# Two early blocks of the first expert, and another order of the experts' turns, in a fused transformer and mixture-of-experts layer

## The chip, the cores and the metric

The kernel runs on one core of a Trainium2 chip. The metric is the device time of one execution in microseconds (us). A core has a matrix engine (TensorE, PE in the rows; its weight loads are PEld), a vector engine (VectorE, DVE), an activation engine (ScalarE, ACT), a general engine (GpSimd, POOL) and a queue engine that issues most transfers (SyncE, SP). Each runs its own instructions in a fixed order, and they wait for each other through semaphores.

## The reference, cut to what matters

One layer on 2,048 tokens of width 1,024: attention and a gated MLP are mixed and projected, the result is normalised and modulated (h2), and h2 goes through a mixture of 32 experts of which each token uses two. What an expert does with its tokens:

```python
    def run_block(args):
        xt, e = args
        hid = jax.nn.silu(xt @ w1[e]) * (xt @ w3[e])
        return hid @ w2[e]
    y = lax.map(run_block, (xb, blk_e)).reshape(cap, d)
    out = jnp.zeros_like(t).at[buf_tok].add(y * buf_w[:, None])
    ...
    x = _layernorm(ALPHA * x + g2 * _hier_moe(h2, lp), ln2_g[i], ln2_b[i])
```

Each expert has 6 MB of weights in fp32 (w1, w3: 1,024 x 512, w2: 512 x 1,024).

## The kernel before

`pass1` computes the projections and the attention, `pass2` the mixing, the norms and the routing of the tokens, `moe` the experts, `final` the last norm. Routing writes, for each expert, a list of its tokens and their weights to `tok_d`; `moe_tables` ranks the experts by their number of tokens, and `CAPS` says how many rows each rank computes (448 down to 64; what does not fit goes through a slow loop, `further_blocks`).

**The end of pass2.** `first_expert` picks the expert that has the most tokens in the first twelve of sixteen token tiles. `early_block` takes 128 of its tokens, which are known before the routing ends, and puts their work between that of the last four tiles (`last_tiles`): it gathers their rows of h2, multiplies by w1 and w3 in plain fp32 (L987, tiles `mm<-mraw,ex`), gates, multiplies by w2, scales (`result`, L1029) and adds into `acc_d`. The order of this stretch is made by a planner (`Plan`) from hand-given durations. The expert's list is then moved forward by 128 places, so that `moe` sees only the rest.

**The turns of moe.** `ORDER` lists the ranks in the order in which they get their turn; rank 0 is the expert of the early block. A turn has one to four blocks of 128 rows; where the rows of a rank end on 64, the last block has 64 rows. For each block i the program runs `hidden(i)` (48 matmuls of 128x512, 32 for a 64-row block), the transposes of the gate of block i-1, `gate(i)` (silu on ACT, products on DVE), `rows(i+1)` (8 transposes of the next block's gathered rows, split into a high and a low part), `output(i-1)` (24 matmuls, or 16) and `evacuate(i-1)` (DVE scales the result, for 64 rows GpSimd also multiplies by g2, then a GpSimd transfer adds the rows into `acc_d`).

**The weights.** An expert's weights come as six pieces of 1 MB into eight buffers `mraw` (RAWS = 8). `prepare` splits each piece into a high part (`mWh`, a cast on ACT) and a low part (`mWl`, a subtraction on DVE, both at L84) and then issues the next load. There are six places for split pieces, so pieces 0 to 3 of the next expert are split during the last block of this one, as `hidden` gives their places free, and pieces 4 and 5 in the block after, behind `output`:

```python
            if last:
                prepare(s + 1, 3)
            if i and blocks[i - 1][3]:
                prepare(s, 4)
                prepare(s, 5)
```

**The start of moe.** SP reads the ranked experts' numbers, loads the token lists (L1519, which waits until the last of the routing's writes to `tok_d` has landed) and two weight pieces (L1530); GpSimd gathers three blocks of rows (L1565); `rows(0)` needs the first of them. The tiles: `xg` gathered rows, `xh`/`xl` their split transposes, `hs` the gated hidden rows, `gh`/`gl` their split transposes, `yo` a scaled result. L1579 and L1586 are the transposes of 128-row and 64-row blocks, L1600 is every matmul of an expert.

Of the kernel before, what the change touches and what calls it, by code (L numbers as in the profile page):

```python
# [703 lines left out]
def pass2(k):  # L704
    nc, tc, T = k.nc, k.tc, k.T
    k.late = k.ctx.enter_context(tc.tile_pool(name="late", bufs=1, reuse_waits="tile"))
    with ExitStack() as ctx:
# [245 lines left out]
        def early_block(plan, ends, done):  # L953
# [4 lines left out]
            lst = k.late.tile([P, 2], I32, name="elst")  # L958
            nc.sync.dma_start(lst, k.tok_d[bass.ds(e, 1), 0:P, :].rearrange("o p w -> p (o w)"))
# [58 lines left out]
            turn, take = rows(lambda: E["hs"], 0, (wk, "vg", 2))  # L1018
# [6 lines left out]
            def result(h):  # L1025
                if h == 0:
                    E["yo"] = k.late.tile([P, D], F32, name="eyo", tag="yo", bufs=1)
                sl = slice(h * 512, (h + 1) * 512)
                nc.vector.scalar_tensor_tensor(E["yo"][:, sl], E["y", h], lst.bitcast(F32)[:, 1:2], E["g2"][:, sl],  # L1029
                                               op0=OP.mult, op1=OP.mult)  # L1030

            def store():
                tc.keep_in_program_order(nc.gpsimd.indirect_dma_start(
                    out=k.acc_d[0:(nb + 1) * P, :], out_offset=bass.IndirectOffsetOnAxis(ap=lst[:, 0:1], axis=0),
                    in_=E["yo"], in_offset=None, compute_op=OP.add))
            d = [add("DVE", 0.65, lambda h=h: result(h), d) for h in range(2)]
            add("Pool", 1.0, store, *d, *done[:4])

# [458 lines left out]
def moe(k):  # L1497
    nc, tc, T = k.nc, k.tc, k.T
    with ExitStack() as ctx:
# [32 lines left out]

        def prepare(s, p):
# [336 lines left out]
```

## Time and profile before

| | |
|---|---|
| median of 3 runs | 2368.75 us (2363.58 to 2372.4) |
| the profiled execution | 2368.24 us, span of its instructions 2366.1 us |
| PE busy | 2206.7 us, 93% of the span |
| DVE, ACT, GpSimd busy | 1739.7, 1196.1, 662.7 us |
| weight pieces of the experts | 192 of 1,024 KB |
| first and last transposes and matmuls of moe | 1496.15 us, about 2303 us |

A busy time is the sum of an engine's instructions; how much of it can be shortened is told only by the rows of one stretch, which stand below.

### The profile page before, as it was taken

Reading aid. Unit: us, or ns where it says so; the run is one execution under the profiler, and the core shown is the slowest. Engines: PE = TensorE matmul, PEld = TensorE weight load, DVE = VectorE, ACT = ScalarE, POOL = GpSimd, SP = SyncE. Lnnn points to the kernel's source line nnn. Section 1 sums busy time; section 2 is a strip of 40 time slices with the busy share of each in tenths; the row PEclk is TensorE's granted clock in tenths of the full one; section 3 lists DMA queues with packets and bytes.
Section 4 is the critical chain, followed back from the end, with each engine's and each line's share of the span. In section 5 each row is a group of like instructions: output and inputs, shape, how many; then the busy total and the mean of one; then the engine's idle time right before and its main releaser. Section 6 shows DMA issues by size and latency. Waiting matters only on the chain. (4 is left out here: it accounts for less than half of the span.)

```text
span 2366.1 us, 31837 instructions
## 1 busy us (share of the span) xinstructions
PE 2206.7 (93%) x11269; PEld 1811.8 (77%) x11269; DVE 1739.7 (74%) x3029; ACT 1196.1 (51%) x1673; POOL 662.7 (28%) x518
## 2 busy tenths in 40 slices
PE   7899999999999999999999998899999998999980
PEld 3799898897788788878877886677777786777770
DVE  4778888887675777578557858489786968658977
ACT  3566666666332334333333333367665756546655
POOL 1333333331000101011101113234363636224424
PEclk9999999999999999999999998899999999999995
DMA  8111111115574445544445435699998989768967
GB/s 311 63 59 59 59 54 41 41 46 198 186 245 139 160 147 178 156 143 152 134 127 162 148 94 191 209 329 340 303 352 273 332 246 334 252 195 310 361 184 293
DMA packets 126853, 449.86 MB, mean 190 GB/s; under 512 B 20778, under 2 KB 42210, under 8 KB 102116
## 3 DMA queue, kind: packets, MB, share of 16 engines
q1 hardware_dynamic: 113828, 405.82, 49.2%
q0 software_dynamic: 12864, 41.98, 7.8%
q8 instruction: 90, 1.47, 0.2%
q14 instruction: 71, 0.58, 0.1%
HBM read 383.18 MB, written 64.57 MB: 189 GB/s over the span
## 5 line engine op out<-in xcount | busy, mean ns | idle before, releaser
L84 DVE TENSOR_TENSOR mWl<-mraw,mWh 128x2048 fp32r<-128x2048 f32 x192 | 437.5, 2311 | 57.6 <-ACT mWh L84 56.8
L84 ACT CAST mWh<-mraw 128x2048 fp32r<-128x2048 f32 x192 | 360.2, 1912 | 108.5 <-PE h L1600 79.1
L99 POOL TENSOR_TENSOR mv<-mv,mhalf 128x1 f32<-128x1 f32 x58 | 60.2, 1040 | 663.7 <-DVE mv L98 657.4
L84 DVE TENSOR_TENSOR Wl<-raw,Wh 128x1024 fp32r<-128x1024 f32 x140 | 170.5, 1220 | 77.4 <-ACT Wh L84 77.0
L1600 PE MATMUL h<-mWh,xh 128*128 128x512 f32 x784 | 217.9, 398 | 3.8 <-ACT xh L84 2.5
L84 ACT CAST Wh<-raw 128x1024 fp32r<-128x1024 f32 x140 | 146.1, 1048 | 139.6 <-PE mm L742 67.3
L1600 PE MATMUL h<-mWl,xh 128*128 128x512 f32 x784 | 210.9, 390 | 0.0
L741 PE MATMUL mm<-hh,Wl 128*128 128x512 f32 x512 | 201.8, 394 | 6.6 <-DVE Wl L84 6.6
L740 PE MATMUL mm<-hh,Wh 128*128 128x512 f32 x512 | 203.3, 397 | 2.5 <-ACT Wh L84 1.9
L742 PE MATMUL mm<-hl,Wh 128*128 128x512 f32 x512 | 201.5, 393 | 0.0
L1647 POOL DMA_INDIRECT acc_d<-yo,lst x49 | 141.3, 2883 | 194.0 <-DVE yo L1641 132.4
L1600 PEld LDWEIGHTS h<-mWl,xh 128*128 128x128 f32 x784 | 147.5, 188 | 31.7
L1600 PEld LDWEIGHTS h<-mWh,xh 128*128 128x128 f32 x784 | 144.2, 189 | 35.1 <-ACT xh L84 3.3
L1646 POOL TENSOR_TENSOR yo<-yo,g2b 64x1024 f32<-64x1024 f32 x20 | 119.9, 5997 | 127.4 <-DVE yo L1644 119.6
L382 PE MATMUL pj<-wq,hTh 128*128 128x256 f32 (+1 forms) x544 | 150.3, 352 | 1.7 <-DVE hTh L363 1.6
L1600 PE MATMUL h<-mWh,xl 128*128 128x512 f32 x464 | 126.7, 394 | 5.5 <-DVE xl L84 5.4
L84 ACT CAST ph<-pt 128x512 fp32r<-128x512 f32 x184 | 93.4, 520 | 73.3 <-PE pt L571 69.8
L547 ACT ACTIVATE Sb<-Sb,mx 128x641 f32<-128x641 f32 (+1 forms) x128 | 105.4, 823 | 40.5 <-DVE mx L542 31.5
L1600 PE MATMUL y<-mWh,gh 128*128 128x512 f32 x392 | 112.7, 407 | 13.1 <-DVE gh L84 11.7
L540 DVE CUSTOM_DVE_ANT_0 Sb<-S,mask,sink 128x640 f32<-128x640 f32 (+1 forms) x128 | 110.3, 862 | 18.9 <-PE S L536 16.1
L84 DVE TENSOR_TENSOR pl<-pt,ph 128x512 fp32r<-128x512 f32 x184 | 109.1, 605 | 19.1 <-ACT ph L84 17.2
L1565 POOL DMA_INDIRECT xg<-h_d,lst x49 | 76.9, 1569 | 163.2 <-PE tr L1579 81.3
(379 smaller groups left out, 5393.1 us busy)
## 6 DMA issues: line engine op xcount, KB each, us to landing
mraw<-mw SPq DMA_DIRECT2D x192, 1024.0 KB
raw<-wf SPq DMA_DIRECT2D x96, 512.0 KB
raw<-ada SPq DMA_DIRECT2D x32, 512.0 KB
raw<-wo SPq DMA_DIRECT2D x32, 512.0 KB
x<-x SPq DMA_DIRECT2D x30, 512.0 KB
x<-ada SPq DMA_DIRECT2D x16, 512.0 KB
hT_d<-hf SPq DMA_DIRECT2D x32, 256.0 KB
raw<-hT_d SPq DMA_DIRECT2D x16, 512.0 KB
```

The lines of the kernel that those rows point to most:

```text
L84: return k.nc.scalar.copy(hi, src), (eng or k.nc.vector).tensor_sub(lo, src, hi)
L99: nc.gpsimd.tensor_tensor(mv[:, 3:4], mv[:, 2:3], k.mhalf, op=OP.pow)
L382: ins = nc.tensor.matmul(box[0][:, :n], x[:, kc, ts], wpart(y, kc, slice(c0, c0 + n))[:, 0, :], start=q == 0, stop=q == 3 * KC - 1)
L540: nc.vector.tensor_tensor_reduce(x[:, :nk], S[:, :nk], mask[:, mi, :nk], 1.0, sink[:, h:h + 1], OP.add, OP.max, mx[:, s:s + 1])
L547: nc.scalar.activation(Sb[s][:, :nk + 1], Sb[s][:, :nk + 1], AF.Exp, bias=mx[:, 2 + s:3 + s], scale=1.0, accum_out=mx[:, 4 + s:5 + s])
L740: nc.tensor.matmul(out, lh, rh, start=first, stop=False)
L741: nc.tensor.matmul(out, ll, rh, start=False, stop=False)
L742: nc.tensor.matmul(out, lh, rl, start=False, stop=last)
L1565: ins = nc.gpsimd.indirect_dma_start(out=xg[i][0:n, :], out_offset=None, in_=k.h2_d[:, :], in_offset=bass.IndirectOffsetOnAxis(ap=lists[s] ...
L1600: nc.tensor.matmul(accs[m], a[:, ks], b[:, c0:c0 + 512], start=first and i + j == 0, stop=last and j == 1 and i == len(t) - 1)
L1646: nc.gpsimd.tensor_tensor(yo[0:64], yo[0:64], g2[0:64], op=OP.mult)
L1647: nc.gpsimd.indirect_dma_start(out=k.acc_d[:, :], out_offset=bass.IndirectOffsetOnAxis(ap=l[0:n, j, 0:1], axis=0), in_=yo[0:n, :], in_offs ...
```

## The change

1. `early_block` loads and gathers 256 tokens of the first expert: the first 128 into `xg` as before, the next 128 into a tile of their own, `k.xg0`. The list is moved forward by 256 places, and the rows of rank 0 go from 384 to 256.
2. The second half of the early block's work (the product with w2, its scaling and its store) leaves `early_block` and becomes `early_output` at the start of `moe`. Its operand waits in `k.early`, in one of the eight `mraw` buffers; so one weight piece fewer is loaded at the start of `moe`, and it follows in the second block's step.
3. The second 128 tokens become block 0 of `moe`, whose rows come from `k.xg0`. `moe` has 49 blocks as before, and `pass2` works on one.
4. Places of tiles: the split pieces get a place each by their number, and some tiles are named first, which sets where they lie in memory.
5. In a turn of more than two blocks with 64 rows left over, the block of 64 rows comes second and not last.
6. Another `ORDER`.

```diff
             e = nc.sync.value_load(k.e0[0:1, 0:1], min_val=0, max_val=31)
-            lst = k.late.tile([P, 2], I32, name="elst")
-            nc.sync.dma_start(lst, k.tok_d[bass.ds(e, 1), 0:P, :].rearrange("o p w -> p (o w)"))
+            k.elst = k.late.tile([P, 2, 2], I32, name="elst")
+            nc.sync.dma_start(k.elst, k.tok_d[bass.ds(e, 1), 0:2 * P, :].rearrange("o (b p) w -> p (o b) w", p=P))
...
-            nc.sync.dma_start(rest, move(1))
+            nc.sync.dma_start(rest, move(2))
             nc.sync.dma_start(move(0), rest)
             xg = whole(wk, "rr", 4)
-            nc.gpsimd.indirect_dma_start(out=xg, out_offset=None, in_=k.h2_d[0:(nb + 1) * P, :],
-                                         in_offset=bass.IndirectOffsetOnAxis(ap=lst[:, 0:1], axis=0))
+            k.xg0 = k.late.tile([P, D], F32, name="xg0", tag="yo", bufs=1)
+            for b, x in enumerate((xg, k.xg0)):
+                nc.gpsimd.indirect_dma_start(out=x, out_offset=None, in_=k.h2_d[0:(nb + 1) * P, :],
+                                             in_offset=bass.IndirectOffsetOnAxis(ap=k.elst[:, b, 0:1], axis=0))
...
-                E["g2"] = whole(wk, "rr", 4)
-                nc.sync.dma_start(E["g2"], bcast_row(k.g2_d[0], D))
...
-            d = add("ACT", 0.5, take, d, w[6], *done[4:])
-            for kc in range(4):
-                for m in range(2):
-                    d = add("PE", 0.87, lambda kc=kc, m=m: product("y", m, 0, kc, k.raws[0, 4 + kc // 2][:, (2 * (kc % 2) + m) * 512:(2 * (kc % 2) + m + 1) * 512]), d)
...
+            def take():
+                k.early = k.mr.tile([P, 2048], F32, name="early", tag="mraw", bufs=RAWS)
+                nc.scalar.copy(k.early[:, D:D + 512], E["t", 0])
...
-CAPS = [384, 448, 384, 320, 320, 256, 256] + [192] * 4 + [128] * 8 + [64] * 13
+CAPS = [256, 448, 384, 320, 320, 256, 256] + [192] * 4 + [128] * 8 + [64] * 13
-ORDER = [0, 20, 14, 7, 16, 22, 6, 25, 9, 13, 19, 3, 27, 10, 15, 28, 2, 24, 29, 30, 4, 23, 1, 31, 8, 11, 17, 26, 5, 18, 21, 12]
+ORDER = [0, 20, 5, 22, 6, 25, 7, 11, 19, 3, 27, 8, 12, 24, 4, 28, 9, 14, 30, 2, 23, 10, 16, 29, 1, 26, 13, 15, 31, 17, 21, 18]
...
-        blocks = []
+        blocks = [(0, None, P, False)]
         for s, r in enumerate(ranks):
             nb = -(-CAPS[r] // P)
-            for j in range(nb):
+            js = list(range(nb))
+            if nb > 2 and CAPS[r] % P == 64:
+                js.insert(1, js.pop())
+            for j in js:
                 n = P if CAPS[r] - j * P > 64 else 64
-                blocks.append((s, j, n, j == nb - 1))
+                blocks.append((s, j, n, j == js[-1]))
...
+        def early_output():
+            y = [bank("y", 2) for _ in range(2)]
+            yo, x, l = k.early[:, 0:D], k.early[:, D:D + 512], k.elst[:, 0, :]
+            for kc in range(4):
+                for m in range(2):
+                    nc.tensor.matmul(y[m], x[:, kc * P:(kc + 1) * P],
+                                     raws[0, 4 + kc // 2][:, (2 * (kc % 2) + m) * 512:(2 * (kc % 2) + m + 1) * 512],
+                                     start=kc == 0, stop=kc == 3)
+            for h in range(2):
+                sl = slice(h * 512, (h + 1) * 512)
+                nc.vector.scalar_tensor_tensor(yo[:, sl], y[h], l.bitcast(F32)[:, 1:2], g2[:, sl], op0=OP.mult, op1=OP.mult)
...
+        xg[0] = k.xg0
+        rows(0)
+        early_output()
         list_load(0)
-        gather(0)
         gather(1)
         gather(2)
         list_load(1)
-        for _ in range(RAWS - 6):
+        for _ in range(RAWS - 7):
             load()
...
-        for p in range(4):
-            prepare(0, p)
-        rows(0)
-        for p in (4, 5):
+        gather(3)
+        for p in range(6):
             prepare(0, p)
```

**PE at the start of moe.** The first row is the last product of the ranking of the experts, which ends pass2's part; `ex` and `early` hold the early block's gated rows. Before:

```order
L1418 MATMUL tr<-R,pc 1x32
L987 MATMUL mm<-mraw,ex 128x512 x8
L1579 MATMUL tr<-ident,xg 128x128 x8
L1600 MATMUL h_14877<-mWh,xh 128x512
L1600 MATMUL h_14878<-mWh,xh 128x512
```

And with the change, where `xg_13923` is the tile `k.xg0` and the second row of transposes is that of block 1, gathered at the start of moe:

```order
L1406 MATMUL tr<-R,pc 1x32
L1577 MATMUL tr<-ident,xg_13923 128x128 x8
L1654 MATMUL y<-mraw,early 128x512 x8
L1598 MATMUL h_14886<-mWh,xh 128x512
...
L1598 MATMUL h_14887<-mWh,xh 128x512
L1577 MATMUL tr<-ident,xg 128x128 x8
L1598 MATMUL h_14886<-mWl,xh 128x512
```

The transposes that wait for a gather of moe now stand behind those of the early gather, the early product and 16 matmuls of block 0 (12 with the first piece, 4 with the second).

**DVE at the same place.** The first row writes the experts' numbers in order of rank, for which SP waits. Before:

```order
L1420 CAST eor<-tr 1x32
L1029 SCALAR_TENSOR_TENSOR eyo<-mm,elst,err 128x512 x2
L84 TENSOR_TENSOR mWl<-mraw,mWh 128x2048 x6
L84 TENSOR_TENSOR xl<-tr,xh 128x512 x2
L1618 TENSOR_TENSOR hs<-hs,h_14878 128x512
```

With the change:

```order
L1408 CAST eor<-tr 1x32
L84 TENSOR_TENSOR xl<-tr,xh 128x512 x2
L84 TENSOR_TENSOR mWl<-mraw,mWh 128x2048 x2
L1659 SCALAR_TENSOR_TENSOR early<-y,elst,g2b 128x512 x2
L84 TENSOR_TENSOR mWl<-mraw,mWh 128x2048 x4
L84 TENSOR_TENSOR xl<-tr,xh 128x512 x2
L1616 TENSOR_TENSOR hs<-hs,h_14887 128x512
```

Two of the six subtractions moved ahead of the early block's scaling, and block 0's own split ahead of all six.

**DVE in a run of light turns.** Before, around the second of three successive turns of one 64-row block (ranks 24, 29 and 30):

```order
L1641 SCALAR_TENSOR_TENSOR yo<-y,lst,g2b 128x512 x2
L1625 TENSOR_TENSOR hs<-hs,hq 64x512
L84 TENSOR_TENSOR mWl<-mraw,mWh 128x2048 x5
L1623 TENSOR_TENSOR hq<-hq,h_18552 64x512
L84 TENSOR_TENSOR gh<-tr,gh 128x4x64
L1623 TENSOR_TENSOR hs<-hs,h_18551 64x512
```

With the change, around rank 31, one of the last seven turns (ranks 26, 13, 15, 31, 17, 21, 18), which have one block each:

```order
L84 TENSOR_TENSOR gl<-tr,gh 128x512
L84 TENSOR_TENSOR mWl<-mraw,mWh 128x2048 x4
L1621 TENSOR_TENSOR hs<-hs,h_20697 64x512
L1621 TENSOR_TENSOR hq<-hq,h_20698 64x512
L84 TENSOR_TENSOR xl<-tr,xh 128x512 x2
L84 TENSOR_TENSOR mWl<-mraw,mWh 128x2048
```

Three 64-row turns no longer follow each other anywhere, and the longest row of single-block turns is now the seven at the end (three before).

## Rows read from the trace of the kernel before

**Rows 1.** The page: the span, and the busy time of each engine.

```profile
span 2366.1 us, 31837 instructions
PE 2206.7 (93%) x11269; PEld 1811.8 (77%) x11269; DVE 1739.7 (74%) x3029; ACT 1196.1 (51%) x1673; POOL 662.7 (28%) x518
```

**Rows 2.** The waits of PE from the ranking's last product to the end of moe (1478.55 to 2304.5 us): who waited for whom, us in total, times, longest.

```profile
PE y L1600 <- DVE gh L84: 11.7, 5, 7.6
PE tr L1579 <- DVE gh L84: 9.4, 10, 1.7
```

**Rows 3.** PE in order of time at the start of moe: start us, us, line and instruction, and in brackets the idle time before it and what ended it.

```profile
1478.69 8.83 PE L987 MATMUL mm<-mraw,ex 128*128 128x512 f32 x16
...
1496.15 1.97 PE L1579 MATMUL tr<-ident,xg 128*128 128x128 f32 x8 [8.62 <-DMA xg<-h_d,lst]
1498.03 2.07 PE L1600 MATMUL h<-mWh,xh 128*128 128x512 f32 x4
...
1511.44 1.03 PE L1579 MATMUL tr<-ident,xg 128*128 128x128 f32 x8
1512.71 1.20 PE L1600 MATMUL h<-mWh,xh 128*128 128x512 f32 x4 [0.24 <-ACT xh L84]
```

**Rows 4.** The other engines in the same stretch, in order of time: GpSimd's last write of the routing and its first gather, SP's list loads and weight loads, ACT and DVE.

```profile
1482.00 0.96 POOL L1376 DMA_INDIRECT tok_d<-tokid,idx  x1 [0.30 <-issue]
1488.22 0.97 POOL L1565 DMA_INDIRECT xg<-h_d,lst  x1 [5.26 <-issue]
1485.40 1.54 SPq L1519 DMA_DIRECT2D lst<-tok_d  x3
1487.13 0.86 SPq L1530 DMA_DIRECT2D mraw<-mw  x2
1488.39 9.10 ACT L84 CAST mWh<-mraw 128x2048 fp32r<-128x2048 f32 x5 [9.92 <-issue]
1488.23 13.32 DVE L84 TENSOR_TENSOR mWl<-mraw,mWh 128x2048 fp32r<-128x2048 f32 x6
```

**Rows 5.** The DMA queues from 1488 to 1492.5 us (packets, MB, share of the 16 engines): one row, that of q1, which is SP's queue. The gathers of GpSimd go through q0.

```profile
q1 hardware_dynamic: 257, 1.58, 101.2%
```

**Rows 6.** DVE's groups of instructions between 1512 and 2290 us: line, operation, tiles and shapes, count, busy us and mean ns of one, idle us before them. First the subtraction of a weight piece, then those of a 128-row block, then those of a 64-row block (there are two more like its third row, at L1623).

```profile
L84 DVE TENSOR_TENSOR mWl<-mraw,mWh 128x2048 fp32r<-128x2048 f32 x185 | 422.0, 2312 | 57.6 <-ACT mWh L84 56.8 <-issue 0.4
L1641 DVE SCALAR_TENSOR_TENSOR yo<-y,lst,g2b 128x512 f32<-128x512 f32 x56 | 39.3, 740 | 25.8 <-PE y L1600 21.0 <-issue 4.8
L84 DVE TENSOR_TENSOR xl<-tr,xh 128x512 fp32r<-128x512 f32 x56 | 36.4, 681 | 0.2 <-ACT xh L84 0.2
L1618 DVE TENSOR_TENSOR hs<-hs,h 128x512 f32<-128x512 f32 x28 | 19.1, 684 | 51.5 <-PE tr L1579 25.7 <-ACT hs L1617 25.4
L84 DVE TENSOR_TENSOR gl<-tr,gh 128x512 fp32r<-128x512 f32 x28 | 19.1, 682 | 16.6 <-ACT gh L84 16.6
...
L1644 DVE SCALAR_TENSOR_TENSOR yo<-y,lst,yo 64x512 f32<-64x512 f32 x38 | 26.5, 735 | 0.0
L84 DVE TENSOR_TENSOR xh<-tr,xh 128x512 fp32r<-128x512 f32 x20 | 13.7, 684 | 1.3 <-ACT xh L84 1.3
L1625 DVE TENSOR_TENSOR hs<-hs,hq 64x512 f32<-64x512 f32 x20 | 13.6, 678 | 0.1
L84 DVE TENSOR_TENSOR gh<-tr,gh 128x256 fp32r<-128x256 f32 x19 | 8.0, 420 | 24.6 <-ACT gh L84 24.6
```

**Rows 7.** [...] In order: the second block of rank 1 (128 rows); its last (64 rows); the single 64-row block of rank 31 behind it; the single 128-row block of rank 13, which follows a 64-row block; the 64-row block of rank 19 behind it; the first block of rank 3 behind that; the three 64-row blocks of ranks 24, 29 and 30, of which the first follows 128 rows; and all of moe from its first hidden matmul.

```profile
2066.37:2084.07 17.70, 17.70 (x85) 14.73 (x84) 7.88 (x8) 4.75 (x7) 4.83 (x3) 1.00 0.54 163
2101.88:2116.37 14.49, 14.08 (x70) 11.08 (x68) 12.64 (x11) 10.12 (x9) 4.19 (x2) 1.00 0.77 247
2116.37:2130.84 14.47, 12.78 (x60) 10.17 (x61) 13.11 (x12) 12.62 (x12) 3.86 (x2) 1.00 1.01 344
...
1725.82:1743.65 17.83, 16.74 (x82) 12.98 (x80) 15.87 (x16) 12.31 (x10) 8.40 (x5) 1.00 0.99 315
1743.65:1757.43 13.78, 13.78 (x67) 11.38 (x66) 13.78 (x9) 13.68 (x13) 8.33 (x1) 1.00 1.02 370
1757.43:1775.20 17.77, 16.53 (x78) 12.99 (x76) 12.66 (x15) 7.08 (x9) 11.70 (x3) 1.00 0.95 356
1937.16:1951.05 13.89, 13.84 (x67) 10.90 (x65) 12.41 (x11) 12.07 (x11) 3.86 (x2) 1.00 0.99 318
1951.05:1972.83 21.78, 14.15 (x61) 11.29 (x62) 19.52 (x15) 14.48 (x12) 13.74 (x2) 0.76 1.00 383
1972.83:1986.66 13.83, 12.66 (x62) 10.06 (x60) 13.23 (x9) 13.73 (x13) 8.87 (x1) 1.00 1.02 354
...
1498.03:2304.50 806.47, 773.93 (x3641) 621.60 (x3640) 619.72 (x514) 485.98 (x442) 331.76 (x114) 0.99 0.86 290
```

**Rows 8.** GpSimd in order of time: the same multiplication of a 64-row block by g2 at two places, and one store of rows.

```profile
2152.18 11.57 POOL L1646 TENSOR_TENSOR yo<-yo,g2b 64x1024 f32<-64x1024 f32 x1 [7.82 <-DVE yo L1644]
...
2298.71 2.39 POOL L1646 TENSOR_TENSOR yo<-yo,g2b 64x1024 f32<-64x1024 f32 x1 [4.93 <-DVE yo L1644]
...
1954.80 12.80 POOL L1647 DMA_INDIRECT acc_d<-yo,lst  x1 [6.93 <-DVE yo L1641]
```

**Rows 9.** DMA queues from 1498 us to the end of moe: packets, MB, share of the 16 engines.

```profile
q1 hardware_dynamic: 32058, 194.04, 63.9%
q0 software_dynamic: 11109, 39.29, 21.6%
```

More of the change, by code (lines that the diff above doesn't have):

```diff
@@ L987, in product @@
                 tc.keep_in_program_order(nc.tensor.matmul(E[name, m], E["x", x][:, kc % 4 * P:(kc % 4 + 1) * P], w,
-                                                          start=kc == 0, stop=kc == (7 if name == "h" else 3)))
+                                                          start=kc == 0, stop=kc == KC - 1))
             def late():
@@ L1017, in early_block @@
             d = add("DVE", 0.6, lambda: gate1(1), d)
-            turn, take = rows(lambda: E["hs"], 0, (wk, "vg", 2))
+            turn, _ = rows(lambda: E["hs"], 0, None)
+            def take():
+                k.early = k.mr.tile([P, 2048], F32, name="early", tag="mraw", bufs=RAWS)
+                nc.scalar.copy(k.early[:, D:D + 512], E["t", 0])
             d = add("PE", 0.45, turn, d)
-            d = add("ACT", 0.5, take, d, w[6], *done[4:])
-            for kc in range(4):
-                for m in range(2):
-                    d = add("PE", 0.87, lambda kc=kc, m=m: product("y", m, 0, kc, k.raws[0, 4 + kc // 2][:, (2 * (kc % 2) + m) * 512:(2 * (kc % 2) + m + 1) * 512]), d)
[L1025 to L1037, printed above, removed]
+            add("ACT", 0.5, take, d)
         def last_tiles(yh, yl, wout):
@@ L1531, in load, with weight @@
                               .rearrange("o p n -> p (o n)"))
+        def weight(n, p):
+            return wk.tile([P, 2048], F32R, name="mW" + n, tag=f"mW{n}{p}", bufs=1)
         def prepare(s, p):
@@ L1536, in prepare @@
                 return
-            hi = wk.tile([P, 2048], F32R, name="mWh", tag="mWh", bufs=6)
-            lo = wk.tile([P, 2048], F32R, name="mWl", tag="mWl", bufs=6)
+            hi, lo = (weight(n, p) for n in "hl")
             split(k, hi, lo, raws[s, p])
@@ L1558, in moe, with place @@
         xg, X, G, H, HS, Y = {}, {}, {}, {}, {}, {}
+        def place(i):
+            s, j, n, _ = blocks[i]
+            return k.elst[:, 1, :] if j is None else lists[s][0:n, j, :]
         def gather(i):
@@ L1634, in evacuate @@
             s, j, n, last = blocks[i]
-            l = lists[s]
-            w = l.bitcast(F32)[0:n, j, 1:2]
+            l = place(i)
+            w = l.bitcast(F32)[:, 1:2]
             yo = (k.late if i % 2 else wk).tile([P, D], F32, name="yo", tag="yo", bufs=1)
@@ L1646, in evacuate @@
                 nc.gpsimd.tensor_tensor(yo[0:64], yo[0:64], g2[0:64], op=OP.mult)
-            nc.gpsimd.indirect_dma_start(out=k.acc_d[:, :], out_offset=bass.IndirectOffsetOnAxis(ap=l[0:n, j, 0:1], axis=0),
+            nc.gpsimd.indirect_dma_start(out=k.acc_d[:, :], out_offset=bass.IndirectOffsetOnAxis(ap=l[:, 0:1], axis=0),
                                          in_=yo[0:n, :], in_offset=None, compute_op=OP.add)
+        def early_output():
[9 more added lines that the diff above has]
+                nc.vector.scalar_tensor_tensor(yo[:, sl], y[h], l.bitcast(F32)[:, 1:2], g2[:, sl], op0=OP.mult, op1=OP.mult)
+            nc.gpsimd.indirect_dma_start(out=k.acc_d[:, :], out_offset=bass.IndirectOffsetOnAxis(ap=l[:, 0:1], axis=0),
+                                         in_=yo, in_offset=None, compute_op=OP.add)
         def rows(i):
@@ L1652, in rows @@
                 X[i] = stationary(xg[i], blocks[i][2], KC, "x")
+        bank("tr", 2), bank("y", 2)
+        for n, p in ("h4", "l4", "h5", "l5", "l3"):
+            weight(n, int(p))
+        for n in ("yo", "hq", "hs", "gh", "gl"):
+            wk.tile([P, D if n == "yo" else 512], F32R if n[0] == "g" else F32, name=n, tag=n, bufs=1)
+        nc.sync.dma_start(g2, bcast_row(k.g2_d[0], D))
+        xg[0] = k.xg0
+        rows(0)
+        early_output()
         list_load(0)
-        gather(0)
         gather(1)
@@ L1673, in moe @@
             rows(i + 1)
-            gather(i + GA)
             if i:
+                gather(i + GA)
                 output(i - 1)
@@ L1682, in moe @@
                 prepare(s, 5)
+            if i == 1:
+                load()
             if i > 3:
```

6 lines of the change are left out of this document (3 added, 3 removed).

## The prediction, made before the changed kernel ran

> **What bounds the kernel now.** I read the page's busy times first: PE is busy for 2206.7 of 2366.1 us, so only what PE waits for, and time at a lower clock, can be won without taking matmuls away [rows 1]. The change takes none away, and up to the ranking's last product (just before 1478.69 us) I take the two programs as equal. What remains is moe, and there the reader sees PE busy for 773.9 of 806.5 us, at a mean granted clock of 0.99 [rows 7]: 32.5 us idle and about 8 us of lower clock, some 40 us in all.
>
> Two places hold what the change can move. The first is the start. PE finishes the early product at 1487.5 us, then stands idle for 8.62 us for the first gathered rows, and comes back slowly: the 8 transposes take 1.97 us there and 1.03 us one block later, the first four matmuls 2.07 against 1.20 us, so the second block starts only at 1512.71 us [rows 3]. The chain to that gather is GpSimd's last list write (1482.00), SP's list load behind it (1485.40), the issue of the gather (1488.22) and its landing before 1496.15 us [rows 3, 4].
>
> The second place is DVE. The longest waits of PE in moe name DVE's split of the gate, `gh` [rows 2]. DVE is busy for 619.7 of 806.5 us on average [rows 7], which says little. What counts is one turn: six subtractions of 2.312 us are 13.9 us whatever the turn's length, and a block adds 2x0.740 + 2x0.681 + 0.684 + 0.682 = 4.2 us (128 rows) or 2x0.735 + 0.684 + 3x0.678 + 0.420 = 4.6 us (64 rows) [rows 6]. So DVE needs 18.1 or 18.5 us for a turn of one block. PE needs 17.7 us for 128 rows after 128 (72 matmuls; the row 2066.37) [rows 7]; less its 12 transposes, about 1.5 us by [rows 3], that is 0.225 us a matmul. With 8 matmuls of h and 8 of y fewer per step, 64 rows after 128 need 14.1, 128 after 64 need 15.9, and 64 after 64 need 12.3 us. DVE's deficit per single turn is thus 0.4 (128 after 128), 2.2 (128 after 64), 4.4 (64 after 128) and 6.2 us (64 after 64).
>
> A deficit does not stall PE at once: DVE has some lead behind a turn of several blocks. Two places give its size. Ranks 13 and 19, with the block behind them, took 17.83 + 13.78 + 17.77 = 49.4 us for 15.9 + 14.1 + 15.9 = 45.9: lost 3.5 of a deficit of 6.6, so 3.1 were covered. Rank 31, 64 rows behind 64, took 14.47 for 12.3, and the block before it 14.49 for 14.1: lost 2.6 of 6.2, covered 3.6 [rows 7]. I take 3.3 us for every run of single turns. The run of three (24, 29, 30) then loses 16.8 - 3.3 = 13.5; its three stretches took 49.5 us for 38.7, and a clock of 0.76 in the second belongs to it [rows 7]. That is 10.8, near enough.
>
> **The start.** The second half of the early work moves behind the transposes of the early gather, and the first gather of moe feeds only block 1. So PE has, from 1478.69 us on, 1.03 of transposes, 8.83 of early product, 16 matmuls of block 0 (3.6), and only then the transposes that wait for a gather [rows 3]. The added list and gather of 128 rows lie in pass2; I cost them at nothing since POOL was busy for 662.7 us of 2366.1 [rows 1], and if they are not covered they cost one gather's issue, 0.97 us [rows 4]. What is bought is the 8.62 us and part of the slow restart. Earliest: nothing is waited for, and block 1 starts at 1478.69 + 1.03 + 8.83 + 48x0.225 + 1.03 = 1500.4 us, 12.3 us sooner. The splits would allow it: ACT's five casts took 9.10 us and had stood idle for 9.92 us ahead of them, for the early block's work, and DVE's six subtractions took 13.32 [rows 4]. Latest: the gather lands as before (1496.15), PE waits about 3 us for it, and restarts as slowly. The stretch 1496.15 to 1512.71 is 16.56 us for 1.03 + 10.8 + 1.03 = 12.9 at full pace, so the slow part cost 3.7; 1496.15 + 1.03 + 32x0.225 + 3.7 = 1508.1, 4.6 us sooner. One of the two weight pieces ahead of the gather is issued later now, and between 1488 and 1492.5 us the traffic was SP's queue alone, at full share [rows 5], so the gather should land somewhat sooner, and PE's idle time is shorter. I take the middle, 8.5.
>
> [...]
>
> **The order and the 64-row blocks in the middle.** PE's matmuls are the same in sum, so the gain is that of the runs. Before, each run counted as the sum of its deficits less 3.3: [20,14], [16,22], [13,19] and [15,28] 3.3 each; [25] 1.1; [27], [23] and [31], single 64s behind a block of 64, 2.9 each; [24,29,30] 13.5; [11,17,26] 3.7; [18,21] 1.5. Sum 41.7, against the 40 us of idle and slow time above. After: ranks 3, 4 and 1 end on 128 rows, so that six lone 64s (20, 22, 25, 27, 28, 23) stand behind 128 rows, 1.1 each, 6.6; four pairs [11,19], [12,24], [14,30], [16,29] 3.3 each, 13.2; and the tail [26,13,15,31,17,21] 4.4 + 2.2 + 0.4 + 4.4 + 2.2 + 4.4 - 3.3 = 14.7. Sum 34.5. The gain is 7.2: the triple and the three 64s behind 64 go, and the tail takes half of it back.
>
> Bounds: if the tail's light turns get their lead anew twice more, it costs 8.1 and the gain is 13.8. If the tail has no lead at all, it costs 18.0 and the gain is 3.9; if the clock falls in it besides as at rank 29 (21.78 us at 0.76, so 5.2 us of it), it is -1.3. I take 7.2, since the same rule gave the measured 40.
>
> Transfers stay hidden: a piece takes 63.9% x 806.5 / 185 = 2.8 us, a block's gather and store 21.6% x 806.5 / 49 = 3.6 [rows 9], so a single turn moves 20.3 us of traffic and DVE asks for it in 18.3. Seven such turns run 14 us behind, and eight loaded pieces are a lead of 22 us. If that cover were gone it would cost those 14 us; the four blocks of rank 1 ahead of the tail fill it. The places given to split pieces add no instruction.
>
> **The sum.** 2368.24 (the profiled execution, 0.5 us below the median of the runs) - 8.5 - 7.2 = 2352.5, on the median's footing 2353.0 us.
>
> **Rivals.** (1) The forecast, 2353. (2) The start gives only 4.6 and the tail is dear (gain 3.9 or less): 2368.75 - 4.6 - 3 = about 2361. For it: the gather's chain through SP and GpSimd is not touched [rows 4]. Against it: one piece less ahead of the gather. (3) The start gives all 12.3 and the tail gets its lead anew: 2368.75 - 12.3 - 13.8 = 2343. Against it: the chain again, and that no run of light turns in this trace was cheaper than the rule. (4) Slower: GpSimd becomes the chain in the tail. The 64-row multiply by g2 took 2.39 us behind the last weight piece, but 11.57 us at 2152.18, amid DVE's subtractions; a store took 12.80 [rows 8]. With a gather's issue, 0.97, and the 5.26 us that GpSimd stood at issuing before one [rows 4], that is 30.6 us against DVE's 18.5: 12.1 us late in each of the turns 26, 31 and 21, where the second of two `yo` buffers is not free for DVE, and DVE is what PE waits for. Three of them make 36 us, 2352.5 + 36 = 2389. It decides only where all three are hit (two: 2377), and needs both long values in each; against it, PE's largest waits name DVE and no GpSimd [rows 2], though the triple (24, 29, 30) had that load. (5) The stalls only move: the tail takes all that the triple gave, and PE reaches block 1 no sooner since the splits of pieces are late: 2368.
>
> [...]
>
> **Chances.** (1) 0.58, (2) 0.19, (3) 0.13, (4) 0.06, (5) 0.04. A measurement of this kernel can tell about 0.5% (11.8 us) from no change, so faster means below 2356.9 us: 0.49 of (1) and all of (3), 0.62. Same: 0.09 of (1), with (2) and (5), 0.32. Slower: (4), 0.06. The range reaches from (3), 2343, to the sum with both lower bounds, 2368.75 - 4.6 - 0, or 2364; it leaves out (4), (5) and the far half of (3), under 2 in 10.
>
> **What would show it.** The start is right if the first hidden matmul of block 1 begins between 1500.4 and 1508.1 us, with transposes that wait for the gather behind 16 matmuls and for less than 3 us, and wrong if PE waits there, or for `mWl` or `mWh` in block 0, for more than 5 us. The order is right if the lone 64s behind 128 rows take 14 to 15.5 us each, the four pairs lose about 3 us each, and the tail from rank 26 to the start of rank 18 about 15 us over PE's own time. A wait of PE or DVE on GpSimd's `yo` in the tail speaks for (4); DVE or ACT waiting for `mraw` there means that the transfers' lead was too short. The prediction is wrong if the time before 1478.69 us moves, since I count nothing there, or if the tail loses far from 15 us.

## The result, and the profile after

| | before | changed |
|---|---|---|
| median | 2367.55 us (6 runs) | 2354.20 us (2351.02 to 2358.02, 6 runs) |
| ratio | | 0.9935, 95% interval 0.992 to 0.995 |
| profiled execution: span | 2366.1 us | 2353.3 us |

The change made the kernel faster by 0.65%, about 15 us by the ratio and 13 by the medians; 2353.0 was forecast. The page of the changed kernel, busy times, answers to [rows 1]:

```profile
PE 2207.1 (94%) x11269; PEld 1818.0 (77%) x11269; DVE 1740.1 (74%) x3029; ACT 1196.0 (51%) x1673; POOL 675.2 (29%) x518
```

PE does the same work in a span that is 12.8 us shorter. Two stretches divide the time: from the first hidden matmul of block 1 of moe to the end of the last hidden matmul, and from there to the end of the span. First those of before, then those of after (ends, length, busy us of PE, PEld, DVE, ACT and POOL with the number of instructions, granted clock as a share of full speed, DMA share, GB/s; so in [rows 7]):

```profile
1512.71:2290.41 777.70, 750.05 (x3537) 602.94 (x3538) 608.94 (x504) 480.16 (x433) 322.77 (x111) 0.99 0.86 293
2290.41:2366.10 75.69, 10.48 (x49) 8.10 (x48) 48.73 (x64) 35.27 (x75) 31.24 (x20) 0.62 0.68 240
```

```profile
1503.58:2276.14 772.56, 751.27 (x3538) 607.07 (x3538) 608.09 (x502) 477.96 (x433) 340.07 (x110) 0.99 0.88 300
2276.14:2353.30 77.16, 12.03 (x48) 9.23 (x48) 51.40 (x65) 38.98 (x77) 27.87 (x19) 0.61 0.63 231
```

So block 1 starts 9.1 us sooner, the turns take 5.1 us less, and the end takes 1.5 us more: 12.8 in all. PE at the start of moe (start, us, instruction, in brackets the wait) answers to [rows 3]:

```profile
1477.84 0.26 PE L1406 MATMUL tr<-R,pc 32*1 32x32 f32 x2 [1.45 <-DVE R L1430]
1478.03 1.97 PE L1577 MATMUL tr<-ident,xg 128*128 128x128 f32 x8
...
1486.93 1.49 PE L1598 MATMUL h<-mWh,xh 128*128 128x512 f32 x4
...
1493.81 1.07 PE L1577 MATMUL tr<-ident,xg 128*128 128x128 f32 x8 [2.66 <-DMA xg<-h_d,lst]
1494.64 1.93 PE L1598 MATMUL h<-mWl,xh 128*128 128x512 f32 x4
...
1503.58 1.13 PE L1598 MATMUL h<-mWh,xh 128*128 128x512 f32 x4
```

The wait for a gather is 2.66 us instead of 8.62, and it stands behind 16 matmuls. The waits of PE in the turns now (from 1477.84 to 2293 us; who waited for whom, us in total, times, longest), against [rows 2]:

```profile
PE y L1598 <- DVE gh L84: 9.6, 9, 4.3
PE h L1598 <- DVE xl L84: 9.2, 9, 2.5
PE y L1598 <- DVE yo L1642: 4.1, 1, 4.1
```

And stretches of the turns, as in [rows 7], each from the first hidden matmul of one block to that of the next: ranks 11 and 19 with the first block of rank 3; the single 27 behind rank 3, which now ends on 128 rows; then the run of seven, the blocks of ranks 26, 13, 15, 31, 17 and 21, and the hidden matmuls of rank 18:

```profile
1681.88:1699.41 17.53, 16.72 (x81) 12.97 (x80) 15.58 (x16) 12.31 (x10) 8.33 (x5) 1.00 0.96 294
1699.41:1713.16 13.75, 13.75 (x68) 11.38 (x66) 13.75 (x9) 13.65 (x13) 8.31 (x1) 1.00 1.02 414
1713.16:1730.90 17.74, 16.38 (x81) 12.98 (x80) 12.35 (x14) 6.85 (x8) 11.74 (x3) 1.00 0.91 331
1761.46:1775.21 13.75, 13.75 (x64) 11.45 (x65) 12.48 (x10) 13.04 (x12) 8.09 (x3) 1.00 0.92 319
2155.16:2168.90 13.74, 13.74 (x67) 11.42 (x66) 12.21 (x10) 12.56 (x11) 3.58 (x2) 1.00 1.01 322
2168.90:2183.28 14.38, 12.09 (x57) 9.56 (x56) 14.38 (x12) 10.90 (x8) 9.89 (x1) 1.00 0.97 363
2183.28:2207.18 23.90, 23.90 (x109) 19.41 (x109) 20.47 (x16) 16.63 (x14) 12.57 (x3) 0.93 1.01 365
2207.18:2220.92 13.74, 13.74 (x67) 11.38 (x66) 13.74 (x8) 13.41 (x11) 7.55 (x4) 1.00 0.98 350
2220.92:2247.55 26.63, 19.90 (x82) 15.63 (x80) 23.68 (x19) 14.36 (x11) 11.51 (x2) 0.81 1.02 390
2247.55:2261.28 13.73, 13.73 (x68) 11.38 (x66) 13.08 (x9) 13.63 (x13) 5.49 (x2) 1.00 0.81 285
2261.28:2276.14 14.86, 12.97 (x50) 9.99 (x49) 10.73 (x10) 2.73 (x3) 3.98 (x1) 0.89 0.27 47
```

The first three lose 49.0 - 45.9 = 3.1 us, where the pair of ranks 13 and 19 lost 3.5 before. Rank 27 loses nothing. From rank 26 to the start of rank 18, the stretch for which the prediction gave 14.7, PE takes 106.1 us where its own time by the prediction's prices is 91.8: 14.3 are lost. The hidden matmuls of rank 18, which the prediction did not count, lose 4.1 more (14.86 for 48 x 0.225 = 10.8). The loss sits in ranks 13 and 15 together, 17 and 18, and the stretches of 15, 17 and 18 are the only ones here with a lower granted clock (0.93, 0.81, 0.89). The last six stretches, to which the experiments are compared, take 107.2 us for 88.5: 18.7 are lost.

### The profile page after: what moved, and what is told of

Same layout as the page of the kernel before. It is cut to its first block, busy times and chain, and to the rows that moved or that the text cites. A ratio compares the mean times of both kernels' runs of the same rounds, so it can differ in the third digit from the quotient of the medians.

```text
span 2353.3 us, 31849 instructions
## 1 busy us (share of the span) xinstructions
PE 2207.1 (94%) x11269; PEld 1818.0 (77%) x11269; DVE 1740.1 (74%) x3029; ACT 1196.0 (51%) x1673; POOL 675.2 (29%) x518
## 5 line engine op out<-in xcount | busy, mean ns | idle before, releaser
L1645 POOL DMA_INDIRECT acc_d<-yo,lst x48 | 152.4, 3176 | 187.5 <-DVE yo L1639 89.9
L1644 POOL TENSOR_TENSOR yo<-yo,g2b 64x1024 f32<-64x1024 f32 x20 | 133.0, 6648 | 128.6 <-DVE yo L1642 120.9
L1598 PE MATMUL y<-mWh,gh 128*128 128x512 f32 x392 | 114.7, 409 | 13.7 <-DVE gh L84 9.6
L84 ACT CAST gh<-tr 128x512 fp32r<-128x512 f32 (+1 forms) x65 | 33.2, 521 | 174.2 <-PE tr L1584 113.0
```

The costliest lines, as they stand in the source:

```text
L84: return k.nc.scalar.copy(hi, src), (eng or k.nc.vector).tensor_sub(lo, src, hi)
L1598: nc.tensor.matmul(accs[m], a[:, ks], b[:, c0:c0 + 512], start=first and i + j == 0, stop=last and j == 1 and i == len(t) - 1)
L1644: nc.gpsimd.tensor_tensor(yo[0:64], yo[0:64], g2[0:64], op=OP.mult)
L1645: nc.gpsimd.indirect_dma_start(out=k.acc_d[:, :], out_offset=bass.IndirectOffsetOnAxis(ap=l[:, 0:1], axis=0), in_=yo[0:n, :], in_offset=No ...
```

## The experiments

Times of experiments are given as the ratio to the kernel before on the same chip. The start of moe wanders by some us between executions together with all that lies ahead of it (the ranking's last product came between 1476.2 and 1481.9 us), so single traces are compared by stretches that begin in moe. These repeat well: in the five traces with the new order and the same blocks the turns take 772.2 to 772.8 us.

**Start and order apart.** The changed start with the old order, blocks of 64 last:

```diff
-ORDER = [0, 20, 5, 22, 6, 25, 7, 11, 19, 3, 27, 8, 12, 24, 4, 28, 9, 14, 30, 2, 23, 10, 16, 29, 1, 26, 13, 15, 31, 17, 21, 18]
+ORDER = [0, 20, 14, 7, 16, 22, 6, 25, 9, 13, 19, 3, 27, 10, 15, 28, 2, 24, 29, 30, 4, 23, 1, 31, 8, 11, 17, 26, 5, 18, 21, 12]
-            if nb > 2 and CAPS[r] % P == 64:
-                js.insert(1, js.pop())
```

> The changed start with the old order of turns and the 64-row blocks last. Theory A (start and order are two separate gains): block 1 starts near 1503.6 us as in the changed kernel, every turn behind it costs what it cost in the kernel before, and the time is 9 us under the kernel before, about 2358.5 (ratio 0.996). Theory B (the start only moves a stall: DVE, which splits the first pieces, is later in relation to PE, and the first run of light turns gives it back): block 1 starts near 1503.6 too, but the turns of ranks 20 and 14 lose several us more than in the kernel before, and the time is 2362 or more.

And the kernel before with the changed `ORDER` and with the 64-row block second in turns of more than two blocks:

> The new order and the 64-row block second, with the old start. Theory A by the sum of the prediction: 7.2 us under the kernel before, 2360.4. By the two traces (the runs of light turns lose 40.3 before and 35.2 after, and the changed kernel loses 1.5 us behind the last hidden matmul): 3.6 us, 2364. Theory B (the order does nothing by itself): 2367.5. Block 1 starts at about 1512.7 us in all of them.

Measured: 0.9962 (0.9947 to 0.9976) and 0.9958 (0.9943 to 0.9974). The two stretches of the start alone, then of the order alone:

```profile
1502.28:2280.01 777.73, 750.00 (x3538) 602.99 (x3538) 607.32 (x502) 477.74 (x433) 318.19 (x110) 0.99 0.88 297
2280.01:2358.60 78.59, 13.13 (x49) 10.01 (x48) 51.40 (x65) 38.99 (x77) 27.88 (x19) 0.60 0.64 230
```

```profile
1516.08:2288.32 772.24, 749.70 (x3537) 605.56 (x3538) 611.48 (x504) 480.19 (x433) 347.07 (x111) 0.99 0.86 295
2288.32:2362.50 74.18, 10.50 (x49) 8.11 (x48) 47.29 (x64) 35.26 (x75) 29.63 (x20) 0.61 0.69 245
```

By these stretches the parts add up. Block 1 starts 25.9 us behind the ranking's last product with the new start alone and 34.8 with the new order alone (25.7 with both, 34.2 before). The turns take 777.7 us with the old order, whatever the start, and 772.2 to 772.6 with the new: theory A, and nothing of the start is given back in the first run of light turns. The whole times are blunter: 0.9962 x 0.9958 = 0.9920, at the edge of the changed kernel's interval. The end takes 75.7 us before, 74.2 with the new order, 78.6 with the new start and 77.2 with both: the order gains 1.5 there, and something in the code of the start costs 3.

**What the end pays.** A part of the new start's code that still acts at the end is the place that each split piece got by its number. PE's first matmuls of the last product in the changed kernel:

```profile
2286.01 0.70 PE L1598 MATMUL y<-mWh,gh 128*128 128x512 f32 x2 [4.15 <-DVE yo L1642]
```

and what ACT does ahead of it:

```profile
2276.62 0.37 ACT L84 CAST gh<-tr 128x256 fp32r<-128x256 f32 x1 [12.07 <-PE tr L1584]
...
2278.78 3.72 ACT L84 CAST mWh<-mraw 128x2048 fp32r<-128x2048 f32 x2 [1.29 <-issue]
```

ACT idles for 12 us and casts the last two pieces only while the product of the expert before, which reads their places, is under way (it begins at 2277.51 us). The next kernel gives these two pieces the places of the last expert's first two:

```diff
-            hi, lo = (weight(n, p) for n in "hl")
+            hi, lo = (weight(n, p - 4 if s == NE - 1 and p > 3 else p) for n in "hl")
```

> The changed kernel in which the last two pieces of the last expert take the places of its own first two pieces (free since block 48's hidden matmuls), as the kernel before let them, and not those of their number, which the product of the expert before still reads. Theory A (the places by number cost time at the end): ACT casts both pieces during the last hidden matmuls, PE does not wait 4.15 us for DVE ahead of the last 24 matmuls, these end 13 to 14 us behind the last hidden matmul instead of 17.2, and the time is 2 to 3 us under the changed kernel. Theory B (the longer end has another cause, such as DVE's lag from the run of seven light turns): the same time, and PE waits there as before.

Beside it ran the changed kernel once more:

> The changed kernel once more, beside the two below on the same chip. The time should lie 13 to 15 us under the kernel before; from the start of block 1 to the end of the last hidden matmul 772.6 us, as in its first trace, and from there to the end of the span 77.1.

Measured: 0.9931 (0.9918 to 0.9944) and 0.9946 (0.9932 to 0.9960), medians 2352.66 and 2355.58 us. The second of ACT's two casts, PE and the two stretches with the places changed, and then the stretches of the changed kernel's second trace:

```profile
2269.44 1.92 ACT L84 CAST mWh<-mraw 128x2048 fp32r<-128x2048 f32 x1 [2.45 <-PE h L1598]
...
2281.82 0.73 PE L1598 MATMUL y<-mWh,gh 128*128 128x512 f32 x2 [1.35 <-ACTq L1719]
...
1502.05:2274.80 772.75, 751.49 (x3538) 607.11 (x3538) 612.28 (x504) 481.71 (x435) 345.69 (x110) 0.99 0.88 299
2274.80:2348.90 74.10, 10.48 (x48) 8.10 (x48) 47.29 (x64) 35.27 (x75) 29.65 (x20) 0.62 0.69 245
```

```profile
1502.31:2274.78 772.47, 751.09 (x3538) 606.94 (x3538) 608.18 (x502) 477.98 (x433) 343.54 (x110) 0.99 0.88 300
2274.78:2352.10 77.32, 12.07 (x49) 9.25 (x48) 51.40 (x65) 38.99 (x77) 27.87 (x19) 0.61 0.63 231
```

Both casts (the first at 2265.10 us) lie in the hidden matmuls again, the wait of 4.15 us is 1.35, and the end is 3.2 us shorter than in the second trace, with the same turns: theory A.

**Where the 64-row block stands.** The changed kernel with the 64-row block last (the two lines of `js.insert` taken out):

> The changed kernel with the 64-row block of ranks 3, 4 and 1 last again. Theory A (what counts is which block stands ahead of a light turn): ranks 27, 28 and 26 stand behind 64 rows, each with a deficit of 6.2 instead of 4.4 us, so 5.4 us more than the changed kernel, about 2359.5; PE waits for DVE in the turns of 27 and 28 as it did in the kernel before (2.2 us each). Theory B (a turn of several blocks gives DVE lead enough either way): 2354, as the changed kernel.

And with the 64-row block first also in turns of two blocks:

```diff
-            if nb > 2 and CAPS[r] % P == 64:
-                js.insert(1, js.pop())
+            if nb > 1 and CAPS[r] % P == 64:
+                js.insert(nb > 2, js.pop())
```

> The changed kernel with the 64-row block of ranks 7, 8, 9 and 10 (two blocks) first, so that ranks 11, 12, 14 and 16 stand behind 128 rows. Theory A: the four pairs lose 0.4 + 4.4 - 3.3 = 1.5 us instead of 3.3 each, 7.2 us less than the changed kernel, about 2347. Theory B (the stall moves into the turn of two blocks, whose first block is now 64 rows behind 64 rows, 12.3 us of PE, with the last two pieces to be split in it): 2354 or more, with PE waiting for DVE in the first block of ranks 7 to 10.

Measured: 0.9944 (0.9928 to 0.9960) and 0.9925 (0.9909 to 0.9940), both within the changed kernel's interval (0.992 to 0.995), so the traces decide. Rank 27 and the turns as a whole with the block last:

```profile
1762.24:1776.73 14.49, 12.81 (x61) 10.18 (x62) 13.12 (x12) 12.64 (x12) 3.81 (x2) 1.00 1.00 334
...
1502.58:2280.66 778.08, 752.79 (x3538) 605.67 (x3538) 607.63 (x502) 477.80 (x433) 335.21 (x110) 0.99 0.88 298
```

5.5 us more for 5.4 expected: theory A. With the block first:

```profile
1502.56:2274.34 771.78, 752.28 (x3538) 607.39 (x3538) 619.27 (x502) 479.60 (x433) 294.43 (x110) 0.99 0.89 301
```

That is only 0.8 less than 772.56. The stretch from rank 27 to the first block of rank 4 shows why: ranks 12 and 24 and the block behind them get cheaper (18.02 + 13.75 + 17.27 us for 47.7 of PE's own, where it was 17.88 + 13.74 + 17.75 for 45.9), but the turns of 27 and 8 ahead of them now take 14.40 + 13.46 + 16.39 for 42.3 instead of 13.75 + 16.34 + 13.75 for 44.1. The whole is 93.29 us against 93.21. The pair loses 1.3 us, as the rule said (1.5), and the loss moved to the 64-row block that now stands behind the single 64, and to that single: theory B.

**Even runs.** With that rule of blocks and seven pairs, two single 64s, one pair of 64s and three turns at the end:

```diff
+ORDER = [0, 11, 20, 5, 12, 22, 6, 13, 25, 7, 14, 19, 3, 27, 8, 15, 24, 4, 28, 9, 16, 30, 2, 23, 29, 10, 17, 26, 1, 18, 21, 31]
```

> The changed kernel with the 64-row block first also in turns of two blocks, and the light turns spread evenly: seven pairs of 128 and 64 rows, each behind a block of 128, two single 64s, one pair of 64s (ranks 23, 29) and ranks 18, 21, 31 at the end. Theory A by the rule of deficits less 3.3: 7 x 1.5 + 2 x 1.1 + 7.3 + 1.5 = 21.5 us instead of 34.5, 13 us less than the changed kernel, about 2341. Theory B (the sum of the deficits counts, whatever the runs, since turns of several blocks give DVE no lead that it keeps): about 2354.

Measured: 0.9945 (0.9932 to 0.9958), no gain over the changed kernel, as theory B said. The turns as a whole, that of rank 29, and DVE and PE in it:

```profile
1506.03:2280.36 774.33, 753.26 (x3546) 607.86 (x3546) 616.44 (x500) 476.89 (x429) 289.72 (x109) 0.99 0.89 299
2089.06:2111.70 22.64, 15.04 (x60) 11.97 (x61) 20.18 (x15) 14.79 (x12) 13.74 (x2) 0.77 1.01 384
...
2093.05 11.09 DVE L84 TENSOR_TENSOR mWl<-mraw,mWh 128x2048 fp32r<-128x2048 f32 x5
...
2105.12 2.08 PE L1598 MATMUL y<-mWh,gh 128*128 128x512 f32 x4 [7.60 <-DVE gh L84]
```

But it is not theory B's reason, a sum that counts wherever it stands. Six of the seven pairs of 128 and 64 rows lose 1.3 to 1.9 us with the block behind them, near the rule's 1.5. The loss is dear where 64 rows follow 64: ranks 23 and 29 lose 36.5 - 26.4 = 10.1 us (7.3 by the rule), and the pair of ranks 13 and 25 with the 64-row block behind it 49.6 - 44.1 = 5.5. In the turn of 29 five subtractions stand in DVE's order ahead of the `gh` that PE waits for, as ahead of rank 29 before, where PE's longest wait was also 7.6 us [rows 2]. PE's granted clock is 0.77 in this turn, and it takes 22.64 us for 12.3. In this turn the place in DVE's order and the clock behind the wait thus cost more than the work in sum tells.

**DVE's work, and GpSimd's.** The changed kernel without the subtraction of piece 5 in turns of one block, and without the multiplication by g2 on GpSimd:

```diff
+            if p == 5 and CAPS[ranks[s]] <= P:
+                nc.scalar.copy(hi, raws[s, p])
+                lo = hi
```

> The changed kernel without the subtraction of the last piece in turns of one block (its low part is left out, and the high part stands in its place in the matmuls; PE, ACT and the transfers do what they did). Theory A (DVE's work in a single turn sets the pace): DVE needs 16.2 us for a 64-row and 15.8 for a 128-row turn instead of 18.5 and 18.1, the deficits are 2.1, -0.1 and -1.9, no run reaches 3.3, and nearly all that the light turns lose goes: 25 to 33 us less than the changed kernel, 2321 to 2329. Theory B (ACT's casts, the transfers or GpSimd set it): within 5 us of the changed kernel, 2349 to 2354.

```diff
-            if n < P:
-                nc.gpsimd.tensor_tensor(yo[0:64], yo[0:64], g2[0:64], op=OP.mult)
```

> The changed kernel without GpSimd's multiplication of the 64-row blocks by g2 (left out of the result). Theory A (GpSimd is not on the path): 2352 to 2355. Theory B (GpSimd holds up DVE's subtractions, some of which take 3.9 instead of 2.27 us in the changed kernel, and that counts in the runs of light turns): the mean subtraction falls from 2.32 to about 2.28 us and the time to 2341 to 2349.

Measured: 0.9893 (0.9877 to 0.9908), some 10 us under the changed kernel and between the two theories, and 0.9922 (0.9905 to 0.9938), which the time alone does not tell from the changed kernel. The traces tell more. From rank 13 to the last hidden matmul the changed kernel takes 107.2 us; the first takes 91.5 there and the second 100.9. The turn of 17 and all turns of the first, and then all turns of the second:

```profile
2229.86:2247.02 17.16, 16.04 (x81) 13.06 (x80) 16.70 (x16) 13.50 (x12) 6.17 (x1) 1.00 1.01 407
...
1505.16:2272.40 767.24, 749.12 (x3542) 606.49 (x3542) 575.57 (x483) 477.74 (x435) 250.20 (x110) 0.99 0.88 303
```

```profile
1506.20:2271.87 765.67, 746.64 (x3538) 603.84 (x3538) 600.37 (x502) 477.64 (x433) 260.75 (x91) 1.00 0.89 302
```

In the long run DVE's work is the cause: with 2.3 us less of it per turn and the same DMA share, 15.8 of the 18.7 us go, and PE's clock there is 1.00. But all turns together gain only 5.3, since the four pairs elsewhere cost more, three of them 3.0 us each, and the fourth 1.9 with the block ahead of it. In the pair of 12 and 24 DVE takes 10.51 us for the same four subtractions that took 8.88, ahead of an `xl` for which PE now waits 2.20 us instead of 0.43. What made them longer stands on GpSimd. Its multiplication of a 64-row block by g2 just ahead of rank 12, in the changed kernel and then without the subtraction, with DVE's four:

```profile
1796.54 11.56 POOL L1644 TENSOR_TENSOR yo<-yo,g2b 64x1024 f32<-64x1024 f32 x1 [7.78 <-DVE yo L1642]
```

```profile
1797.28 4.54 POOL L1648 TENSOR_TENSOR yo<-yo,g2b 64x1024 f32<-64x1024 f32 x1 [5.58 <-DVE yo L1646]
1800.07 10.51 DVE L84 TENSOR_TENSOR mWl<-mraw,mWh 128x2048 fp32r<-128x2048 f32 x4
```

The first of the four takes 3.90 us here, and it is the one beside the multiplication. In all, GpSimd's 20 multiplications fall from 133.0 to 69.1 us, and DVE's mean subtraction rises from 2.326 to 2.380 us. So DVE's work was not simply taken away: where it grew lighter, GpSimd's multiplication was done sooner and a subtraction took longer.

GpSimd takes part in the changed kernel too: without its multiplication the run from 13 on is 6.3 us shorter and the turns 6.9. Six subtractions of the turns take 2.8 to 4.4 us, each beside a multiplication, two of them in that run (the first at 2206.70 us, 3.88 instead of 2.27); without the multiplication none does. It holds the other way as well: the multiplication takes 2.36 to 2.40 us at each of the six places of the changed kernel's trace where no subtraction runs beside it, and 11.55 to 11.58 us at each of the eight where just four do. By what mechanism the two lengthen each other is not shown. On average a subtraction takes 2.284 us without the multiplication and 2.326 with it, by the two rows, without and with it:

```profile
L84 DVE TENSOR_TENSOR mWl<-mraw,mWh 128x2048 fp32r<-128x2048 f32 x186 | 418.8, 2284 | 66.4 <-ACT mWh L84 65.9
```

```profile
L84 DVE TENSOR_TENSOR mWl<-mraw,mWh 128x2048 fp32r<-128x2048 f32 x186 | 426.8, 2326 | 65.2 <-ACT mWh L84 64.7
```

**The weight piece ahead of the gather.** Its load is issued behind the split of the first piece:

```diff
-        for _ in range(RAWS - 7):
-            load()
...
         for p in range(6):
             prepare(0, p)
+            for _ in range(RAWS - 7 if p == 0 else 0):
+                load()
```

> The changed kernel with the load of the one weight piece ahead of the gathers of moe issued only with the split of the first piece. Theory A (SP's weight pieces hold up GpSimd's gather): the gathered rows of block 1 land some 2.7 us sooner, PE's wait of 2.66 us ahead of the transposes goes and the slow matmuls behind it with it, 3 to 4 us less than the changed kernel, about 2350.5. Theory B (the gather waits for its own chain, the list load and the issue): the transposes start at 1493.8 us as before, 2354.

Measured: 0.9947 (0.9933 to 0.9961), no gain. The rows landed 1494.47 - 1480.36 = 14.1 us behind the ranking's last product, against 1493.81 - 1477.84 = 16.0 in the changed kernel, so a piece ahead of the gather does hold it up, by 1.9 us. It is not scatter: in the ten traces with the changed start as it is, the rows landed 15.7 to 16.1 us behind that product. GpSimd's issue of the gather, in the changed kernel and then with the load later:

```profile
1487.46 0.98 POOL L1563 DMA_INDIRECT xg<-h_d,lst  x1 [5.20 <-issue]
```

```profile
1490.03 0.98 POOL L1563 DMA_INDIRECT xg<-h_d,lst  x1 [5.26 <-issue]
```

From this issue to the landing it is 7.9 us with two pieces ahead (before, [rows 3, 4]), 6.4 with one and 4.4 with none. (A piece is 2.8 us of traffic, the prediction's estimate from [rows 7, 9], so this run shows a delay, of 2.0 us, but not of a whole piece.) But the order of PE's work moved as well, and the transposes stand behind 4 matmuls instead of 16:

```profile
1494.47 1.94 PE L1577 MATMUL tr<-ident,xg 128*128 128x128 f32 x8 [3.56 <-DMA xg<-h_d,lst]
```

PE waits 3.56 us instead of 2.66, and block 1 starts 26.4 us behind the ranking's last product instead of 25.7. What the sooner landing is worth with the old order of PE stays open.

**A shorter run at the end.** With the places of last_places, three of the 128-row experts move ahead of single 64s:

```diff
+ORDER = [0, 13, 20, 5, 15, 22, 6, 17, 25, 7, 11, 19, 3, 27, 8, 12, 24, 4, 28, 9, 14, 30, 2, 23, 10, 16, 29, 1, 26, 18, 21, 31]
```

> The same with another order: the 128-row experts 13, 15 and 17 go from the last seven light turns ahead of the single 64s 20, 22 and 25 near the beginning, and the end is ranks 26, 18, 21, 31. Theory A (a long run of light turns costs DVE's lead and more, a pair behind 128 rows 1.9 us, as the pairs of the evenly spread order did): three pairs for three single 64s cost 4 us more, the run at the end 8 instead of 17.5, so moe takes 5 us less than with last_places and the time is 7 to 8 us under the changed kernel. Theory B (the deficits count in sum, or ranks 21 and 31, 64 rows behind 64, stall as ranks 24 and 29 did, by some 10 us): no gain over last_places.

Measured: 0.9911 (0.9898 to 0.9925), median 2348.88 us beside 2355.58 of the changed kernel on the same chip: 6.7 us less. The turns and the end:

```profile
1505.56:2273.17 767.61, 749.61 (x3546) 605.66 (x3546) 609.96 (x502) 478.96 (x431) 340.58 (x109) 1.00 0.89 301
2273.17:2349.20 76.03, 10.13 (x40) 7.51 (x40) 49.29 (x66) 37.61 (x79) 32.98 (x21) 0.60 0.66 235
```

4.9 us less in the turns, theory A; of the 3.2 us that the places give back the end keeps 1.1. The last block now has 64 rows, with more to do behind its product, which may be why; no run parts this. It is the fastest version here that leaves nothing out.

## Why the prediction was right, step by step

**The start** was right in mechanism. The ranking's last product to block 1 took 1512.71 - 1478.55 = 34.2 us before [rows 3] and takes 25.7 now, 8.4 less for 8.5 forecast; the gather is waited for behind 16 matmuls, for 2.66 us where less than 3 was said, and it landed sooner by the piece that is no longer ahead of it. That the size fits to a tenth is luck: 8.5 was the middle of two bounds, and in four of the ten traces with this start the same stretch took 23.9 to 24.2 us. The rest of the 9.1 is the ranking's last product, which came 0.7 us sooner, within its scatter.

**The order** was right in sum (7.2 forecast; 5.1 in the turns and 1.5 at the end, 6.6), and its two large terms were met: the pairs lose 3.1 to 3.5 us each for 3.3, and the tail from rank 26 to the start of rank 18 14.3 for 14.7. DVE's deficit is what the tail costs (five_lows), and which block stands ahead of a single 64 counts as forecast (half_last). Three terms were off, and that they cancel is luck. The six single 64s lose 0.7 us in all with the blocks behind them, where 6.6 was said: each takes 13.7 to 13.8 us, under the 14 to 15.5 that was to be the sign. The hidden matmuls of rank 18 lose 4.1, and were not counted. The three 64-row turns of the kernel before were priced at 13.5 by the rule and at 10.8 by their own rows, so the argument against rival (3), that no run was cheaper than the rule, did not hold. (A slip without effect: 64 rows have 16 hidden matmuls fewer than 128, not 8; the times that follow are worked out with 16.)

The rule itself, DVE's deficit less one cover of 3.3 us a run, reaches less far than the experiments took it. Their expectations of 7 us (half_first) and 13 (even_runs) gave 0.8 and -1.8: pairs behind 128 rows met it, but it has no term for a 64-row block at the head of a turn of two, and too small a one for a pair of single 64s. It also takes the subtraction at a fixed 2.312 us. In half_first the mean is 2.386 and in even_runs 2.368, while GpSimd's 20 multiplications fall from 133.0 us to 67.6 and 61.9; how much of the missing gain that takes stays open.

**The places by number** were the term that was mis-sized: "add no instruction" was taken as no cost. They cost 3.2 us at the end of moe, where no next expert wants the pieces' places. With that term the sum would have been 2368.24 - 8.5 - 7.2 + 3.2 = 2355.7.

**Transfers** stayed hidden, as costed: in the turns of the changed kernel no wait of PE, ACT or DVE names the load of a weight piece.

**Rival (4)**, GpSimd in the tail, was real in a smaller form. It does not queue up so that DVE waits for a `yo`; it is DVE's subtractions that take longer, six of them 2.8 to 4.4 us instead of 2.27 beside GpSimd's multiplication. The turns lose 6.9 us by it (no_g2), inside a forecast that had priced the subtractions at their mean.

## What to carry to other kernels

An engine's busy time in a step told here when a long run of light steps would stall (14.3 us lost for 14.7 forecast); in a single step, look also for what stands in its queue behind a block of long instructions (7.60 us of waiting behind five subtractions in even_runs), and ask whether a cure moves the wait into the step ahead. Do not take an instruction's time as fixed where two engines lengthen each other, as a subtraction (2.27 to 4.4 us) and a multiplication (2.36 to 12.17 us) did here: work taken from one can come back through the other. When tiles get fixed places, look at the last round, where a free place used to be taken (3.2 us here). Spread light steps out, keep two of the lightest apart, and time each part of a change by a stretch that begins and ends inside it.

## What was not expected of the hardware

PE's restart behind the same wait came out in two ways: in the changed kernel the first matmuls behind the gather took 1.93 us at a granted clock of 0.83 for the stretch to block 1, and in half_first, with the same instructions and a wait of 2.51 us, 1.17 at 1.00; block 1 then starts 24.1 instead of 25.7 us behind the ranking's last product. The difference ahead of it is that the first transposes, 16 us earlier, took 1.97 us in the one and 1.09 in the other. The ten traces with this start divide by it: where those transposes took 1.09 to 1.52 us (four traces), block 1 starts 23.9 to 24.2 us behind the ranking's last product; where they took 1.76 to 1.97 (six), 25.7 to 25.9. What sets it stays open.
